# Where the tiles that TensorE reads lie in SBUF: multiples of 256 bytes instead of multiples of 32

## The chip, the core and the metric

The kernel runs on one core of a Trainium2 chip. The metric is device time in microseconds of one execution of the whole program; three executions of the kernel before were timed.

## What is computed

One layer of a hybrid decoder trunk: u is the RMS-normed input (16 meta tokens and 2,048 real ones, 1,024 features); one projection of u gives all inputs of two branches, a Mamba-2 scan (SSD) and gated linear attention (GLA), and the gates that merge them; then come the branch projections, the gated sum, the output projection and a last RMS norm.

```python
u = rmsnorm(hres, norm_w)
proj = jnp.einsum('bld,dn->bln', u, w_in)
z, xbc, dt_raw, q, k, v, g_gla, a_lr, merge_g = split_cols(proj, IN_WIDTHS)
...
y_m, s_m = ssd_chunked(xs[:, :m], dt[:, :m], a, bm[:, :m], cm[:, :m], N_META, s0)
y_r, _ = ssd_chunked(xs[:, m:], dt[:, m:], a, bm[:, m:], cm[:, m:], SSD_CHUNK, s_m)
...
o_r, _ = gla_chunked(q[:, m:], k[:, m:], v[:, m:], log_a[:, m:], GLA_CHUNK, st_m)
...
branch_proj = jnp.einsum('blnc,ncd->blnd', branches, w_branch)
gates = jax.nn.sigmoid(merge_g.reshape(b, l, N_BRANCH, D_MODEL))
merged = jnp.sum(gates * branch_proj, axis=2)
return hres + jnp.einsum('bld,de->ble', merged, w_out)
```

## The kernel before

**Matrix products.** Nearly all products are made from fp32 values split in two: a high half rounded to fp32r and a low half, the rest. A tile holds both halves side by side, `[P, 2, n]`, and `accum` (L212 to L216) makes three matmuls of them: high by high (L214), high by low (L215), low by high (L216). The stationary operand has 128 columns, the moving one up to 512. Each matmul loads its own weights.

**First phase.** The 2,048 tokens go in four blocks of 512; block 0 also holds the 16 meta tokens, so its tiles have 528 columns and the real tokens start at column 16. u of a block is eight tiles (one for each 128 features): blocks 1 and 3 use tiles named `uo`, blocks 0 and 2 tiles named `ue`, which have room for 528 columns in each half (`u_tile`, L267). `proj_feat` (L218) streams u past weights (moving u, stationary `whl`), `proj_tok` (L230) streams weights past u. Block 0's projections over all 528 columns go in two segments of 264 (L407), each in a PSUM bank of its own. The scans of both branches run beside the projections; their small products read tiles named `act`, `sq`, `c1`, `tok4`, `kdt`, `atp`, `bt`.

**Second phase.** Gates, branch projections and the output projection are done with seven products of sums and differences for eight (a Strassen-like scheme). For each pair of halves, `prep_a` (L1160) splits a stationary tile `a`, `prep_b` (L1112) a moving tile: `b6`, `b7`, `b5`, `b3`, `b4`, or, for products 1 and 2, one of the `ue` tiles again. `product` (L1168) runs four k-steps of three matmuls of 512 columns, in the order of products 1, 2, 6, 7, 5, 3, 4, each for two row groups: 168 matmuls for two row groups in all.

**Order.** TensorE's and SyncE's instructions run in the order in which the code is written (a manual schedule); those of the other engines are placed by a scheduler that models their times.

**Addresses.** Tiles come from pools. Left of the free gap, the pools follow each other upward from the end of the scratch for software DMAs (16 KiB a partition); right of it, downward from the top of SBUF. A tile starts on a multiple of 32 bytes; nothing more is asked for. So where a tile lies past a multiple of 256 bytes follows from the sizes of all pools ahead of it. For the tiles that TensorE reads most:

| Tile | read as | start past a multiple of 256 bytes: first half / second half |
|---|---|---|
| `uo` (blocks 1, 3) | moving and stationary | 96 / 96 |
| `ue` (blocks 0, 2, products 1 and 2), even and odd tiles | moving and stationary | 160 / 224 and 32 / 96 |
| `whl` (weights of the first phase) | moving and stationary | 96 / 96 |
| `a` (second phase) | stationary | 160 / 160 |
| `b6` | moving | 160 / 160 |
| `b7`, `b5`, `b3`, `b4` | moving | 224 / 224 |
| `sq`, `c1`, `kdt`, `atp`, `ot` | both | 32 |
| `act` | both | 32, 96, 160 or 224 |

In block 0 the real tokens add 64 bytes to this (16 columns), and the second segment adds 1,056 bytes, 32 past a multiple of 256.

**Software DMAs.** Eight DMAs of the whole program are issued by GpSimd (L346, block 0's u to DRAM). GpSimd also makes the low halves of the weights (L177, L190), which TensorE waits for.

Of the kernel before, what the change touches and what calls it, by code (L numbers as in the profile page):

```python
# [8 lines left out]
F32 = mybir.dt.float32  # L9
# [34 lines left out]
def trunk_kernel(ctx: ExitStack, tc: tile.TileContext, xm, xmt, w_feat, w_tok, w_v3, w_zm, w_br, w_o,  # L44
# [11 lines left out]
    base = ctx.enter_context(tc.tile_pool(name="base", bufs=1))  # L56
    wdram = ctx.enter_context(tc.tile_pool(name="wdram", bufs=1, space=bass.MemoryType.DRAM))
    dpool = ctx.enter_context(tc.tile_pool(name="dpool", bufs=2, space=bass.MemoryType.DRAM))
    mhalf = base.tile([P, 4], F32, name="mhalf")
    nc.vector.memset(mhalf, -0.5)  # L60


# [61 lines left out]
    def pool1(name, bufs):  # L124
        return first.enter_context(tc.tile_pool(name=name, bufs=bufs, side="right"))

    bpool, wk, sm, const = pool1("bpool", 1), pool1("wk", 2), pool1("sm", 4), pool1("const", 1)
    pj = ctx.enter_context(tc.tile_pool(name="pj", bufs=3, space=bass.MemoryType.PSUM))
    pt = ctx.enter_context(tc.tile_pool(name="pt", bufs=3, space=bass.MemoryType.PSUM))
    pc = ctx.enter_context(tc.tile_pool(name="pc", bufs=2, space=bass.MemoryType.PSUM))  # L130

    def bank(pool, tag):
        return mk(pool, [P, 512], F32, tag)
# [3 lines left out]
    ident = cst[:, 0, :]  # L137
    tri = cst[:, 1, :]
    tris = cst[:, 2:4, :]
    pv = const.tile([P, 118], F32, name="pv")  # L140
    norm_w = pv[:, 0:8]
    conv_w = pv[:, 8:72].rearrange("p (t k) -> p t k", k=4)
    conv_b = pv[:, 72:88]
# [121 lines left out]


    def u_tile(b):  # L267
        return mk(uodd, [P, 2, BLK], F32R, "uo") if b % 2 else mk(ueven, [P, 2, META + BLK], F32R, "ue")

    def load_u(b):  # L270
        m0 = META if b == 0 else 0
        row0 = META - m0 + b * BLK
        tt = m0 + BLK
        u = []

        def rows_load(r0, n, i=None):
            xt = mk(wk, [P, D], F32, "tok4", bufs=NT4) if i is None else mk(spool, [P, META + BLK], F32, "acc")[:, :BLK]
            nc.sync.dma_start(xt[:n], xm[r0:r0 + n, :] if i is None else xm[r0:r0 + n, i * BLK:(i + 1) * BLK])
            return xt

        def rstd_rows(ss, n):
            r = mk(sm, [P, 1], F32, "rs1")
            nc.vector.tensor_scalar(r[:n], ss[:n], 1.0 / D, EPS, op0=ALU.mult, op1=ALU.add)
            done = nc.gpsimd.tensor_tensor(r[:n], r[:n], mhalf[:n, 0:1], op=ALU.pow)
            return (r, done) if m0 else r

        def rows_rstd(r0, n, vector):
            ss = mk(sm, [P, 1], F32, "ss")
            xt = rows_load(r0, n)
            if vector:  # L290
                nc.vector.scalar_tensor_tensor(xt[:n], xt[:n], 1.0, xt[:n], op0=ALU.mult, op1=ALU.mult,
                                               accum_out=ss[:n])
            else:
                nc.scalar.activation(xt[:n], xt[:n], AF.Square, accum_out=ss[:n])
            return rstd_rows(ss, n)

        rs = []
        if m0:
            rm_s = rows_rstd(0, META, True)
            for c in range(NCH):  # L300
                rs.append(rows_rstd(META + b * BLK + c * P, P, c % 2))
        else:
            for c in range(NCH):
                s2 = mk(sm, [P, 2], F32, "ss2")
                for i in range(2):
                    xt = rows_load(META + b * BLK + c * P, P, i)
                    nc.scalar.activation(xt, xt, AF.Square, accum_out=s2[:, i:i + 1])
                    if i == 0:
                        yield
                ss = mk(sm, [P, 1], F32, "ss")  # L310
                nc.vector.tensor_tensor(ss, s2[:, 0:1], s2[:, 1:2], op=ALU.add)
                rs.append(rstd_rows(ss, P))
                yield
        if m0:
            rs.append(rm_s)
            first_rows.append(rs[NCH - 1][1])
            rs = [r for r, _ in rs]
            nc.sync.dma_start(cst[:, :2], cf32[:, :2])
            nc.sync.dma_start(pv, pvec)
            for q in range(NWR):  # L320
                raws[f"zm_{q}"] = load_raw(w_zm[:, q * 288:(q + 1) * 288])
        rb = bank(pt, "pt")
        for c in range(NCH):
            nc.tensor.matmul(rb[:, c * P:(c + 1) * P], rs[c].to_broadcast([P, P]), ident, start=True, stop=True)
        rbs = [(rb, m0, BLK)]
        if m0:
            rm = bank(pt, "pt")
            nc.tensor.matmul(rm[:, :META], rs[NCH][:META].to_broadcast([META, P]), ident[:META, :META],
                             start=True, stop=True)
            rbs = [(rm, 0, META)] + rbs  # L330
        else:
            rbc = mk(spool, [P, 3 + META + BLK], F32, "cin")[:, :BLK]
            nc.scalar.activation(rbc, rb, AF.Copy)
            rbs = [(rbc, 0, BLK)]
            yield
        lows = []
        for kt in range(KT):
            xk = (mk(wk, [P, META + BLK], F32, "act", bufs=NACT) if m0 else mk(spool, [P, META + BLK], F32, "acc"))[:, :tt]
            nc.sync.dma_start(xk, xmt[:, kt, row0:row0 + tt])
            with tc.issue_after(lows[kt - 2].ins) if m0 and kt > 1 else nullcontext():  # L340
                for ps, a, n in rbs:
                    nc.vector.scalar_tensor_tensor(xk[:, a:a + n], xk[:, a:a + n], norm_w[:, kt:kt + 1], ps[:, :n],
                                                   op0=ALU.mult, op1=ALU.mult)
            u.append(u_tile(b)[:, :, :tt])
            nc.scalar.activation(u[kt][:, 0], xk, AF.Copy)
            (nc.gpsimd if m0 else nc.scalar).dma_start(u_left[b][kt], xk[:, m0:])  # L346
            lows.append(nc.vector.tensor_tensor(u[kt][:, 1], xk, u[kt][:, 0].bitcast(F32), op=ALU.subtract))
            if m0:
                first_low[:] = lows[:2][-1:]
            yield  # L350
        return u
# [30 lines left out]
    msk = const.tile([P, NMSK, P], U8, name="msk")  # L382

    def late_constants():
        w2r = mk(wk, [P, META + BLK], F32, "act", bufs=NACT)[:48, :512]
        for i in range(3):
            nc.sync.dma_start(w2r[16 * i:16 * i + 16, :], gw2)
        nc.scalar.activation(w2, w2r, AF.Copy)
        nc.vector.tensor_tensor(w2[32:48], w2r[32:48], w2[32:48].bitcast(F32), op=ALU.subtract)
        mstg = mk(wk, [P, D], F32, "tok4", bufs=NT4)[:, :NMSK * P]  # L390
        nc.sync.dma_start(mstg, cmsk)
        nc.vector.tensor_copy(msk.rearrange("p l t -> p (l t)"), mstg)
# [4 lines left out]
    def new_block(b, u):  # L397
# [1 line left out]
        o.b, o.u = b, u  # L399
        o.m0 = META if b == 0 else 0  # L400
        o.tt = o.m0 + BLK
        o.segs_all = [(0, o.tt // 2), (o.tt // 2, o.tt // 2)] if b == 0 else [(0, BLK)]
        o.segs_real = [(o.m0, BLK)]
        o.starts = [o.m0 + c * P for c in range(NCH)]
        o.chunks = ([(0, META)] if o.m0 else []) + [(a, P) for a in o.starts]
# [61 lines left out]

    def gates(o):
        m0, tt, chunks, g_all = o.m0, o.tt, o.chunks, o.g_all
        ast = (mk(wk, [P, META + BLK], F32R, "act", bufs=NACT) if m0 else mk(wk, [P, BLK], F32R, "sq", bufs=NSQ))[:48, :tt]  # L470
        for a, n in ([(0, META), (m0, BLK)] if m0 else [(0, BLK)]):
            ps = bank(pt, "pt")
            for i, (ca, cn) in enumerate(chunks):
# [5 lines left out]
            nc.scalar.activation(ast[:16, a:a + n], ps[:16, :n], AF.Copy)  # L479
        yield  # L480
        for h2 in range(0, GH, 2):
            gmt = mk(wk, [P, 2, META + BLK], F32, "tok4", bufs=NT4)
            for h in (h2, h2 + 1):
                gm = gmt[:, h % 2, :tt]
                gb = gate_b[:, h:h + 1]
# [101 lines left out]
    def proj_conv(o, g):  # L587
        tt = o.tt
        feats = o.feats[g] = []
        for j in range(4):  # L590
# [10 lines left out]
            for k in range(3):  # L601
                convd[:] = [nc.vector.scalar_tensor_tensor(acc, cin[:, k:k + tt], hcw[:, ti, k:k + 1], acc,  # L602
                                                           op0=ALU.mult, op1=ALU.add)]
            f = mk(wk, [P, META + BLK], F32, "act", bufs=NACT)
            nc.scalar.activation(f[:, :tt], acc, AF.Tanh)
            nc.vector.scalar_tensor_tensor(f[:, :tt], f[:, :tt], 1.0, acc, op0=ALU.add, op1=ALU.mult)
            feats.append(f)
# [136 lines left out]

    def proj_qk(o, h):
        t0 = T_GLA + 4 * h
        qs = mk(wk, [P, META + BLK], F32, "act", bufs=NACT)
        ps, = proj_feat(f"g{t0}", w_feat[t0], o.segs_real, o.mov)
        evicted[:] = [nc.scalar.activation(qs[:, :BLK], ps, AF.Copy, scale=QSCALE)]
        yield  # L750
        kf = mk(wk, [P, META + BLK], F32, "act", bufs=NACT)
        for ps, (a, n) in zip(proj_feat(f"g{t0 + 1}", w_feat[t0 + 1], o.segs_all, o.mov), o.segs_all):
            evicted[:] = [nc.scalar.activation(kf[:, a:a + n], ps[:, :n], AF.Copy)]
        o.qk[h] = qs, kf
        yield
# [34 lines left out]
    def gla_scan(o, h, last=False):  # L790
# [5 lines left out]
        k = kf[:, m0:tt]  # L796
        grc = gr.rearrange("p (c t) -> p c t", t=P)

        kd = mk(wk, [P, META + BLK], F32, "act", bufs=NACT)
        gl = mk(sm, [P, NCH + 1], F32, "gl")  # L800
        with behind() if m0 else nullcontext():
            nc.scalar.activation(gl[:, :NCH], grc[:, :, P - 1], AF.Copy, scale=ITEMP)
# [7 lines left out]
        nc.vector.tensor_tensor(kd[:, :tt], kd[:, :tt], kf[:, :tt], op=ALU.mult)  # L810
        egl = mk(sm, [P, NCH], F32, "egl")
        nc.scalar.activation(egl, gl[:, :NCH], AF.Exp)
        qg = mk(wk, [P, META + BLK], F32, "act", bufs=NACT)[:, :BLK]
        nc.scalar.activation(qg, gr, AF.Exp, scale=ITEMP)
        nc.vector.tensor_tensor(qg, qg, q, op=ALU.mult)

# [639 lines left out]
        k += 1  # L1456
    ordered.close()
    first.close()
    bpl.update({p: pool2(f"bops{p}", 4, side="right") for p in (7, 5, 3, 4)})
    opl, spl = pool2("outs", 1, side="right"), pool2("small", 4, side="right")  # L1460
    bt_raws["all"] = opl, "br", 4
# [106 lines left out]
```

## Time and profile before

| | |
|---|---|
| median of 3 timed executions | 2237.41 us (2236.06 to 2238.92) |
| profiled execution: span from first to last instruction | 2236.0 us |
| first phase / second phase in it | up to about 1454 us / from there on |
| instructions | 34,965, of them 11,789 matmuls as the profile counts them |
| DMA | 517.95 MB, mean 232 GB/s |

The page names no other time of the profiled execution than its span. PE is TensorE's matmuls, PEld its weight loads, DVE VectorE, ACT ScalarE, POOL GpSimd, SP SyncE. A row of a timeline has the start in us, the duration in us, engine, source line, operation, the tile written and the tiles read, the shape, and how many instructions were merged in the row. Rows of a list of groups have the count behind an x, then the busy time in us and the mean of one in ns.

### The profile page before, as it was taken

How to read it: one execution, taken by the hardware profiler on the slowest of the kernel's cores; microseconds unless marked ns; L12 is line 12 of the kernel's file. 1: busy time of each engine (PE TensorE's matmuls, PEld its weight loads, DVE VectorE, ACT ScalarE, POOL GpSimd, SP SyncE). 2: the span in 40 equal slices, each digit the busy share in tenths (PEclk: the TensorE clock that was granted, in tenths of full speed). 3: DMA queues.
4: the chain of work that ended last, by engine and by line, in shares of the span. 5: the costliest groups of instructions: out<-in, count | busy, mean ns of one | idle time of the engine just before them, and what ended most of it. 6: DMA issues, size and time to landing. Idle time of an engine off the chain costs nothing.

```text
span 2236.0 us, 34965 instructions
## 1 busy us (share of the span) xinstructions
PE 2209.7 (99%) x11789; PEld 1896.8 (85%) x11789; DVE 1568.4 (70%) x2935; ACT 1187.0 (53%) x2767; POOL 689.2 (31%) x689
## 2 busy tenths in 40 slices
PE   7999999999999999999999999999999999999998
PEld 7999999888888888888988888878888888888887
DVE  5776776677567676567677666774689854789876
ACT  5666655575445466445465454464644545554544
POOL 5444432223212122221212100066233374323341
PEclk9999999999999999999999999999999999999999
DMA  9777775767788667778677664386768866777753
GB/s 318 246 229 240 266 267 192 239 211 237 240 253 258 211 213 236 239 248 269 208 216 230 212 214 157 125 276 202 240 221 288 303 221 212 247 279 248 251 181 120
DMA packets 313699, 517.95 MB, mean 232 GB/s; under 512 B 28080, under 2 KB 162480, under 8 KB 313520
## 3 DMA queue, kind: packets, MB, share of 16 engines
q1 hardware_dynamic: 247008, 419.89, 58.5%
q10 hardware_dynamic: 65872, 93.74, 11.5%
q8 instruction: 92, 1.51, 0.3%
q0 software_dynamic: 640, 2.10, 0.2%
q14 instruction: 87, 0.71, 0.1%
HBM read 368.42 MB, written 147.19 MB: 231 GB/s over the span
## 4 chain that ended last, share of the span: by engine, by line
PE 72%; DMA 1%; DVE 1%; ACT 1%; POOL 0%; issue 0%; POOLq 0%; SPq 0%; ACTq 0%; DVEq 0%
PE pj L214 15%; PE pj L216 15%; PE pj L215 15%; PE pt L214 4%; PE pt L215 4%; PE pt L216 4%; PE pc L216 2%; PE pc L214 2%; PE pc L215 2%; PE pc L691 2%; PE pc L852 1%; PE pc L692 1%; PE pc L960 1%; PE pc L694 1%; PE pt L666 1%; DMA acc<-in_xmt 1%
## 5 line engine op out<-in xcount | busy, mean ns | idle before, releaser
L214 PE MATMUL pj<-ue,whl 128*128 128x264 f32 (+1 forms) x672 | 235.4, 350 | 1.2 <-ACT acc L598 1.2
L216 PE MATMUL pj<-ue,whl 128*128 128x264 f32 (+1 forms) x672 | 229.7, 342 | 0.0
L215 PE MATMUL pj<-ue,whl 128*128 128x264 f32 (+1 forms) x672 | 228.8, 341 | 0.0
L214 PE MATMUL pj<-uo,whl 128*128 128x512 f32 x512 | 205.8, 402 | 0.0
L216 PE MATMUL pj<-uo,whl 128*128 128x512 f32 x512 | 200.2, 391 | 0.0
L215 PE MATMUL pj<-uo,whl 128*128 128x512 f32 x512 | 199.5, 390 | 0.0
L214 PE MATMUL pj<-b,a 128*128 128x512 f32 (+1 forms) x484 | 189.0, 391 | 0.5 <-DVE io L1283 0.5
L216 PE MATMUL pj<-b,a 128*128 128x512 f32 (+1 forms) x484 | 188.9, 390 | 0.0
L215 PE MATMUL pj<-b,a 128*128 128x512 f32 (+1 forms) x484 | 187.6, 388 | 0.0
L602 DVE SCALAR_TENSOR_TENSOR acc<-cin,hcw,acc 128x512 f32<-128x512 f32 (+1 forms) x192 | 157.9, 823 | 39.8 <-ACT acc L598 38.6
L83 POOL TENSOR_TENSOR wr<-wr 128x256 f32<-128x256 f32 x80 | 65.9, 823 | 373.7 <-DMA wr<-y 157.2
L1165 DVE TENSOR_TENSOR a<-ar,a 128x512 fp32r<-128x512 f32 x160 | 136.0, 858 | 61.3 <-ACT a L1164 60.5
L1136 POOL TENSOR_TENSOR as<-ar,ar 128x512 f32<-128x512 f32 x38 | 60.8, 1600 | 371.7 <-DMA ar<-in_w_br 185.9
L214 PEld LDWEIGHTS pj<-ue,whl 128*128 128x128 f32 x672 | 126.4, 188 | 16.7 <-ACT acc L598 1.6
L216 PEld LDWEIGHTS pj<-ue,whl 128*128 128x128 f32 x672 | 126.5, 188 | 14.9
L215 PEld LDWEIGHTS pj<-ue,whl 128*128 128x128 f32 x672 | 126.5, 188 | 14.7
L177 POOL TENSOR_TENSOR whl<-wr,whl 128x512 fp32r<-128x512 f32 (+1 forms) x76 | 96.2, 1274 | 126.0 <-ACT whl L175 80.6
L1199 ACT ACTIVATE sn<-pj 128x512 f32<-128x512 f32 x118 | 69.9, 592 | 121.7 <-PE pj L216 84.4
L1165 DVE TENSOR_TENSOR a<-as,a 128x512 fp32r<-128x512 f32 x120 | 100.6, 840 | 45.0 <-ACT a L1164 42.0
L1164 ACT ACTIVATE a<-ar 128x512 fp32r<-128x512 f32 x160 | 98.8, 624 | 58.1 <-PE pt L216 32.7
L214 PE MATMUL pt<-b,a 128*128 128x512 f32 x320 | 125.7, 393 | 0.0
L215 PE MATMUL pt<-b,a 128*128 128x512 f32 x320 | 125.3, 392 | 0.0
(335 smaller groups left out, 6456.8 us busy)
## 6 DMA issues: line engine op xcount, KB each, us to landing
whl<-k_s SPq DMA_DIRECT2D x96, 512.0 KB, 3.8
whl<-k_g SPq DMA_DIRECT2D x96, 512.0 KB, 4.2
whl<-k_v SPq DMA_DIRECT2D x36, 512.0 KB, 4.0
wr<-in_w_feat SPq DMA_DIRECT2D x64, 256.0 KB, 4.5
k_s<-whl SPq DMA_DIRECT2D x32, 512.0 KB, 3.9
cb<-cumd SPq DMA_DIRECT2D x64, 256.0 KB, 5.1
y<-gg ACTq DMA_DIRECT2D x64, 256.0 KB, 4.0
k_g<-whl SPq DMA_DIRECT2D x32, 512.0 KB, 3.8
```

The lines of the kernel that those rows point to most:

```text
L83: nc.gpsimd.tensor_tensor(o, x, y, op=ALU.subtract)
L177: nc.gpsimd.tensor_tensor(hl[:, 1], raw, hl[:, 0].bitcast(F32), op=ALU.subtract)
L214: nc.tensor.matmul(ps, sh, mh, start=first, stop=False, **kw)
L215: nc.tensor.matmul(ps, sh, ml, start=False, stop=False, **kw)
L216: nc.tensor.matmul(ps, sl, mh, start=False, stop=last, **kw)
L602: convd[:] = [nc.vector.scalar_tensor_tensor(acc, cin[:, k:k + tt], hcw[:, ti, k:k + 1], acc, op0=ALU.mult, op1=ALU.add)]
L666: nc.tensor.transpose(ps[:, j * P:(j + 1) * P], f[:, a:a + P], ident)
L691: nc.tensor.matmul(py[:, h * 64:(h + 1) * 64], dm[:, h], xdt[:, h], start=True, stop=True)
L1136: nc.gpsimd.tensor_tensor(s1, a21, a22, op=ALU.add)
L1164: nc.scalar.activation(t[:, 0], src, AF.Copy)
L1165: latest[:] = [nc.vector.tensor_tensor(t[:, 1], src, t[:, 0].bitcast(F32), op=ALU.subtract)]
L1199: nc.scalar.activation(sn, self.ps[n, "a"], AF.Copy)
```

## The change

It makes every tile that TensorE reads start on a multiple of 256 bytes, in both halves, by padding: `ue` tiles get 576 columns a half instead of 528, `act` tiles 576 instead of 528, the tiles of `gates` 544 instead of 528; four small pads fill pools up. Block 0's two segments become 256 and 272 columns, so that the second starts 1,024 bytes in. For the room, the scratch of software DMAs goes from 16 KiB to 4 KiB a partition. After it the starts of the tiles in the table above are all 0 past a multiple of 256. In block 0 the real tokens still start 64 bytes past that. `g_all` and `alr` (start 32) stay as they were; TensorE reads only `alr` of them, in a few small transposes a block.

```diff
-    mhalf = base.tile([P, 4], F32, name="mhalf")
+    mhalf = base.tile([P, 32], F32, name="mhalf")[:, :4]
...
+    mk(bpool, [P, 8], F32, "pad")
+    mk(spool, [P, 16], F32, "pad", bufs=1)
...
+    def act_tile(dt=F32):
+        return mk(wk, [P, 64 + BLK], dt, "act", bufs=NACT)
...
-    pv = const.tile([P, 118], F32, name="pv")
+    pv = const.tile([P, 128], F32, name="pv")[:, :118]
...
-        return mk(uodd, [P, 2, BLK], F32R, "uo") if b % 2 else mk(ueven, [P, 2, META + BLK], F32R, "ue")
+        return mk(uodd, [P, 2, BLK], F32R, "uo") if b % 2 else mk(ueven, [P, 2, 64 + BLK], F32R, "ue")
...
-        o.segs_all = [(0, o.tt // 2), (o.tt // 2, o.tt // 2)] if b == 0 else [(0, BLK)]
+        o.segs_all = [(0, BLK // 2), (BLK // 2, META + BLK // 2)] if b == 0 else [(0, BLK)]
...
-            gmt = mk(wk, [P, 2, META + BLK], F32, "tok4", bufs=NT4)
+            gmt = mk(wk, [P, 2, 32 + BLK], F32, "tok4", bufs=NT4)
...
-            f = mk(wk, [P, META + BLK], F32, "act", bufs=NACT)
+            f = act_tile()
...
+    top = pool2("top", 1, side="right")
+    mk(top, [P, 56], F32, "pad")
...
-    nc = _bacc.Bacc("TRN2", target_bir_lowering=False, num_devices=1)
+    nc = _bacc.Bacc("TRN2", target_bir_lowering=False, num_devices=1, dynamic_dma_scratch_size=4096)
```

All other places that make an `act` tile use `act_tile` in the same way. Lines of the changed kernel stand 5 lower from there on, and later 7.

TensorE, the first projection of block 0 over all columns, before (pj_621 and pj_622 are the two PSUM banks, ue_313 and ue_321 two tiles of u):

```order
L214 MATMUL pj_621<-ue_313,whl_572 128x264
L215 MATMUL pj_621<-ue_313,whl_572 128x264
L216 MATMUL pj_621<-ue_313,whl_572 128x264
L214 MATMUL pj_622<-ue_313,whl_572 128x264
L215 MATMUL pj_622<-ue_313,whl_572 128x264
L216 MATMUL pj_622<-ue_313,whl_572 128x264
```

and the same place of the changed kernel:

```order
L219 MATMUL pj_623<-ue_315,whl_574 128x256
L220 MATMUL pj_623<-ue_315,whl_574 128x256
L221 MATMUL pj_623<-ue_315,whl_574 128x256
L219 MATMUL pj_624<-ue_315,whl_574 128x272
L220 MATMUL pj_624<-ue_315,whl_574 128x272
L221 MATMUL pj_624<-ue_315,whl_574 128x272
```

The same matmuls stand in the same order, with 256 and 272 columns for 264 and 264; the rest of TensorE's rows are as before, and so are all of GpSimd's and SyncE's. ScalarE, the evictions of block 0's convolution inputs (cin, acc) beside the weights' high halves (whl), before:

```order
L598 ACTIVATE acc_848<-pj_784,hcb,hcw 128x264
L189 ACTIVATE whl_949<-wr_951 128x512
L189 ACTIVATE whl_1021<-wr_1023 128x512
L605 ACTIVATE act_858<-acc_848 128x528
L595 ACTIVATE cin_1213<-tails 128x3
L597 ACTIVATE cin_925<-pj_861 128x264
```

and now:

```order
L603 ACTIVATE acc_850<-pj_786,hcb,hcw 128x272
L194 ACTIVATE whl_951<-wr_953 128x512
L610 ACTIVATE act_860<-acc_850 128x528
L600 ACTIVATE cin_1215<-tails 128x3
L194 ACTIVATE whl_1023<-wr_1025 128x512
L602 ACTIVATE cin_927<-pj_863 128x256
```

One split of a weight moved behind the tanh (L605, now L610) of the convolution before it. A few such moves in block 0 are all that changed in ScalarE's order; VectorE's changed only in the widths.

More of the change, by code (lines that the diff above doesn't have):

```diff
@@ L337, in load_u @@
         for kt in range(KT):
-            xk = (mk(wk, [P, META + BLK], F32, "act", bufs=NACT) if m0 else mk(spool, [P, META + BLK], F32, "acc"))[:, :tt]
+            xk = (act_tile() if m0 else mk(spool, [P, META + BLK], F32, "acc"))[:, :tt]
             nc.sync.dma_start(xk, xmt[:, kt, row0:row0 + tt])
@@ L384, in late_constants @@
     def late_constants():
-        w2r = mk(wk, [P, META + BLK], F32, "act", bufs=NACT)[:48, :512]
+        w2r = act_tile()[:48, :512]
         for i in range(3):
@@ L469, in gates @@
         m0, tt, chunks, g_all = o.m0, o.tt, o.chunks, o.g_all
-        ast = (mk(wk, [P, META + BLK], F32R, "act", bufs=NACT) if m0 else mk(wk, [P, BLK], F32R, "sq", bufs=NSQ))[:48, :tt]
+        ast = (act_tile(F32R) if m0 else mk(wk, [P, BLK], F32R, "sq", bufs=NSQ))[:48, :tt]
         for a, n in ([(0, META), (m0, BLK)] if m0 else [(0, BLK)]):
@@ L746, in proj_qk @@
         t0 = T_GLA + 4 * h
-        qs = mk(wk, [P, META + BLK], F32, "act", bufs=NACT)
+        qs = act_tile()
         ps, = proj_feat(f"g{t0}", w_feat[t0], o.segs_real, o.mov)
@@ L750, in proj_qk @@
         yield
-        kf = mk(wk, [P, META + BLK], F32, "act", bufs=NACT)
+        kf = act_tile()
         for ps, (a, n) in zip(proj_feat(f"g{t0 + 1}", w_feat[t0 + 1], o.segs_all, o.mov), o.segs_all):
@@ L797, in gla_scan @@
         grc = gr.rearrange("p (c t) -> p c t", t=P)
-        kd = mk(wk, [P, META + BLK], F32, "act", bufs=NACT)
+        kd = act_tile()
         gl = mk(sm, [P, NCH + 1], F32, "gl")
@@ L812, in gla_scan @@
         nc.scalar.activation(egl, gl[:, :NCH], AF.Exp)
-        qg = mk(wk, [P, META + BLK], F32, "act", bufs=NACT)[:, :BLK]
+        qg = act_tile()[:, :BLK]
         nc.scalar.activation(qg, gr, AF.Exp, scale=ITEMP)
```

## The prediction

> **What bounds the kernel now.** I read the page from the top: the busy shares, then the chain, then the waits of TensorE, and after these the starts of single matmuls, because nothing else decides here.
>
> ```profile
> PE 2209.7 (99%) x11789; PEld 1896.8 (85%) x11789; DVE 1568.4 (70%) x2935; ACT 1187.0 (53%) x2767; POOL 689.2 (31%) x689
> PE 72%; DMA 1%; DVE 1%; ACT 1%; POOL 0%; issue 0%; POOLq 0%; SPq 0%; ACTq 0%; DVEq 0%
> ```
>
> ```profile
> PE pt L324 <- DMA cst<-in_cf: 10.1, 1, 10.1
> PE pc L691 <- DVE sq L682: 2.0, 2, 1.6
> PE pj L214 <- ACT ue L345: 1.5, 1, 1.5
> ```
>
> TensorE is busy 99% of the span; the chain that ended last is made of matmuls; the longest wait (10.1 us) is the first load, and the next ones together are a few us. So the time is a sum of distances between starts of matmuls, and only what changes these distances changes the time. A matmul's duration in the lists (some 390 ns) is a modelled one that overlaps the next; I therefore use starts, first and last of a run, divided by the number between.
>
> In the second phase (from 1467 us on) TensorE waits for nothing but half a microsecond near the end, and the work repeats every 168 matmuls of 512 columns:
>
> ```profile
> 1660.29 0.39 PE L214 MATMUL pj<-b,a 128*128 128x512 f32 x1
> ...
> 1698.87 0.39 PE L214 MATMUL pj<-b,a 128*128 128x512 f32 x1
> ```
>
> 38.58 us / 168 = **229.6 ns** each. Now a run of the same shape in block 1, whose u lies in tiles "uo", and one in block 2, whose u lies in tiles "ue":
>
> ```profile
> 490.44 0.39 PE L214 MATMUL pt<-whl,uo 128*128 128x512 f32 x1
> ...
> 495.88 0.39 PE L214 MATMUL pt<-whl,uo 128*128 128x512 f32 x1
> ```
>
> ```profile
> 840.46 0.40 PE L214 MATMUL pt<-whl,ue 128*128 128x512 f32 x1
> ...
> 845.33 0.39 PE L214 MATMUL pt<-whl,ue 128*128 128x512 f32 x1
> ```
>
> 24 matmuls in 5.44 us are **226.7 ns** each; 21 in 4.87 us are **231.9 ns**. Engine, line, shape, weights and pools are the same. What differs is where the operands start: uo and whl both at 96 past a multiple of 256 bytes, in both halves; ue at 160 or 32 in the first half and 224 or 96 in the second (4,224 bytes a tile, halves 2,112 apart). The whole blocks say it again, by the first matmul of blocks 1, 2 and 3:
>
> ```profile
> 390.89 0.30 PE L214 MATMUL pj<-whl,uo 128*128 128x288 f32 x1
> 739.65 0.29 PE L214 MATMUL pj<-whl,ue 128*128 128x288 f32 x1
> 1091.79 0.30 PE L214 MATMUL pj<-whl,uo 128*128 128x288 f32 x1
> ```
>
> Block 1 takes 348.8 us and block 2, with the same matmuls, 352.1.
>
> **The change part by part.** The program keeps its instructions; the order on TensorE, GpSimd and SyncE is the same row for row. What moves is the address of nearly every operand, the width of block 0's two segments, and a few evictions.
>
> *Second phase.* Its operands start at 224 (b7, b5, b3, b4), 160 (b6, a) and the four values of ue; after the change all start at 0. One pair there is equal already, b6 with a, 160 and 160 in both halves. It comes behind products of ue, and its first 12 matmuls (1698.87 to the first row here) take 230.8 ns, then it settles:
>
> ```profile
> 1701.64 0.39 PE L214 MATMUL pj<-b,a 128*128 128x512 f32 x1
> ...
> 1704.36 0.40 PE L214 MATMUL pt<-b,a 128*128 128x512 f32 x1
> ```
>
> 12 in 2.72 us, again 226.7 ns, at another start than uo's 96. So I take 226.7 for equal starts, wherever they lie. The matmuls:
>
> ```profile
> L214 PE MATMUL pj<-b,a 128*128 128x512 f32 x476 | 186.7, 392 | 0.0
> L214 PE MATMUL pt<-b,a 128*128 128x512 f32 x320 | 125.7, 393 | 0.0
> L215 PE MATMUL pj<-ue,a 128*128 128x512 f32 x160 | 63.0, 394 | 0.0
> L216 PE MATMUL pc<-ue,a 128*128 128x512 f32 x160 | 63.2, 395 | 0.0
> ```
>
> 1,116 on one line, three lines (high by high, high by low, low by high): 3,348. Times 229.64 - 226.67 = 2.97 ns: **-9.9 us**. All of it is on the path, since nothing else is waited for there. VectorE is next: the window rows give it 269.7 of 383 us and, in the last part, 292.8 of 386, so a phase shorter by 1.3% does not reach it.
>
> ```profile
> 1467.00:1850.00 383.00, 383.00 (x1670) 313.25 (x1669) 269.74 (x348) 194.97 (x347) 181.84 (x142) 1.00 0.74 252
> 1850.00:2236.00 386.00, 378.39 (x1659) 309.68 (x1657) 292.83 (x424) 187.72 (x359) 126.92 (x92) 1.00 0.65 219
> ```
>
> *Blocks 1 and 3* have equal starts already (96) and get others (0): nothing, if only equality counts. *Block 2* becomes like block 1: 3.4 us less, of which a wait that only block 2 has (1.1 us, below) is not the layout's. I take **-2.2 us**.
>
> ```profile
> PE pt L446 <- DVE ecu L443: 1.1, 1, 1.1
> ```
>
> *Block 0* keeps unequal starts: its real tokens stand 16 columns in, 64 bytes past the start of a tile that now is at 0. Its 288 matmuls of 512 columns go from four mixed starts to a pair 64 bytes apart. Such a pair, 224 with 160, are the products of b7, b5 and b3 by a in the second phase:
>
> ```profile
> 1705.06 0.39 PE L214 MATMUL pt<-b,a 128*128 128x512 f32 x1
> ...
> 1717.42 0.39 PE L214 MATMUL pj<-b,a 128*128 128x512 f32 x1
> ```
>
> 54 in 12.36 us, 228.9 ns against 231.9: -0.9 us. Its segments of 264 and 264 columns become 256 and 272:
>
> ```profile
> 54.89 0.28 PE L214 MATMUL pj<-ue,whl 128*128 128x264 f32 x1
> ...
> 56.71 0.28 PE L214 MATMUL pj<-ue,whl 128*128 128x264 f32 x1
> ```
>
> ```profile
> 712.82 0.28 PE L214 MATMUL pj<-whl,uo 128*128 128x256 f32 x1
> ...
> 714.97 0.28 PE L214 MATMUL pj<-whl,uo 128*128 128x256 f32 x1
> ```
>
> 264 columns take 121.3 ns (15 in 1.82 us), 256 with equal starts 119.4 (18 in 2.15 us). A column more costs (226.7 - 119.4) / 256 = 0.42 ns, so 272 take 126.1. The pair goes from 242.6 to 245.5, +2.9 ns, 480 pairs: +1.4 us. A few evictions move by a place with it (ACT is busy 53%); nothing. Block 0 together: **+0.5 us**, between -1 and +2.
>
> *The scratch* for software DMAs shrinks to a quarter. Only block 0's eight stores of u use it:
>
> ```profile
> L346 POOL DMA_DIRECT2D u<-act x8: 539/554/759, 14.0 to 25.9; - x8
> ```
>
> Each holds GpSimd 0.55 us. Behind one that waits for room stands the subtraction that makes a weight's low half, and TensorE waits for that. No row shows such a wait. Its bounds are nothing, and one landing, 4.6 us in the median for this line, for each store that finds no room. I take nothing, by the even 0.54 to 0.76 us of the eight.
>
> *Sum:* 2236.0 - 9.9 - 2.2 + 0.5 = 2224.4 us of span. The page gives that execution no time beside its span; the timed runs' median is 2237.4, 1.4 us above it. Forecast: **2226 us** (2225.8), -0.5%. With block 0's and block 2's bounds, and 228 instead of 226.7 ns in the second phase (-5.5 us), that case spans 2220 to 2232.
>
> **The rivals.**
>
> *The start itself counts, not only its equality.* A matmul of 512 columns at 226.7 ns has 13 ns that are not columns (512 x 0.42 = 214). All starts of these operands are odd multiples of 32 bytes, but for the second segments of block 0, so the trace hardly shows what a multiple of 64 or more would give. If part of the 13 ns is a first or last piece of a line that only a displaced operand has, it goes in all 9,700 or so such matmuls, blocks 1 and 3 too. For it: 13 ns stand there at both widths, as a cost per operand would. Against it: in the 264-column run above every second three start at multiples of 64, and at 121.3 ns it stands only 2 or 3 below 264 x 0.42 + 13 = 124. Half of it, 16 columns or 64 bytes, 6.7 ns: 9,700 x 6.7 = 65 us, so 2161. All of it: 6,800 x 13 = 88 us, and some 8 ns for the 2,800 narrower ones, down to the 111 ns that a pass of 128 columns takes here (8 in 0.89 us), 22 us: 2116.
>
> ```profile
> 633.44 0.89 PE pc L852 x8
> ```
>
> The page "TensorE: Matmul & The Clock Gate" of the Trainium skill, section "Wait — 56ns, not 53.3ns?", gives 512 columns as 215.7 ns back to back; the trace's best run is 11 ns above it. By that figure as a floor, the 3,348 of the second phase alone would lose 47 us, an estimate from that page.
>
> *Nothing.* The difference between uo and ue could come from which buffer is read against which, in steps that alignment to 256 does not touch, or the second phase's 229.6 from its own three PSUM pools. For it: the tiles b have the same start in both halves and still take 228.9. Against it: that start is 64 bytes from a's, and b6, where it is not, settles at 226.7. Time 2237, within 4.5 us.
> The page "SBUF — State Buffer" of the Trainium skill, section "Specifications (TRN2)", has lines of 16 bytes and a penalty for crossing to a new one. Every operand before starts on a multiple of 32 and runs contiguously, so by that rule this change moves nothing; the 226.7 against 231.9 ns above already speak against it as the whole story.
>
> *Slower: equal starts collide.* Weights are loaded while the matmul before streams. If both now begin on the same position of every 256 bytes and position 0 is a bad one, all matmuls take what the worst run takes, 231.9 ns: +2.3 ns on 3,348 and +5.2 on some 2,100 of blocks 1 and 3, which are at 226.7 now: 7.7 + 11 us, and the segments' 1.4: 2258. It decides from a second phase above 230 ns a matmul. For it: at 256 columns equal starts are the slower ones, 119.4 against
>
> ```profile
> 216.57 0.28 PE L214 MATMUL pj<-whl,ue 128*128 128x256 f32 x1
> ...
> 218.69 0.28 PE L214 MATMUL pj<-whl,ue 128*128 128x256 f32 x1
> ```
>
> 117.8 ns for mixed ones (18 in 2.12 us). Against it: at 512 columns equal starts are the fastest that the trace has.
>
> **How the numbers follow.** Equality counts, 2220 to 2232, likeliest 2226: 0.52. The start itself counts: 0.24, of it half the 13 ns or less (2160 to 2220) 0.12, more 0.12. Nothing: 0.13. Slower: 0.11. Below 0.2% (4.5 us, about what a measurement of this kernel can tell from no change) nothing is told apart. So faster 0.76, same 0.13, slower 0.11. The range leaves out the deeper half of the first rival and most of the slower one: 2160 to 2243; the likeliest case's own is 2220 to 2232.
>
> **What would show it.** Right: the period of 168 matmuls in the second phase at 38.1 us (now 38.58), blocks 1, 2 and 3 equally long near 348.8 us, and no new wait of TensorE. Blocks 1 and 3 clearly shorter than now would mean the first rival; a period unchanged, the second; above 38.7 us, the third. A wait of TensorE for a weight's low half before 60 us would mean the scratch. The pairs of block 0 at 245 ns would show the segments' price.

## The result, and the profile after

| | before | changed |
|---|---|---|
| median of the timed executions | 2236.73 us (4 runs, 2233.17 to 2238.92) | 2222.82 us (4 runs, 2221.41 to 2224.33) |
| ratio, 95% interval | | 0.9938 (0.9924 to 0.9952) |
| profiled execution, span | 2236.0 us | 2220.6 us |

The change saves 13.9 us, 0.6%. The profiled execution of the changed kernel itself took 2222.45 us, 1.85 more than its span. If the same 1.85 us are added to the span of before, its profiled execution took about 2237.8 us, an estimate, and lay 1.1 above its median, while the changed one lay 0.4 below its own. So the two spans differ by 15.4 us and the medians by 13.9.

The page of the changed kernel, busy shares and chain: TensorE is still the only engine that decides, and all the others have the load that they had. (The shares of the chain that the page of before lists add up to only 75%, so its 72% for TensorE and the 90% here can't be compared.)

```profile
PE 2194.1 (99%) x11789; PEld 1893.9 (85%) x11789; DVE 1564.9 (70%) x2935; ACT 1186.6 (53%) x2767; POOL 694.4 (31%) x689
PE 90%; DVE 2%; DMA 2%; issue 1%; ACT 1%; POOL 0%; SPq 0%; POOLq 0%; ACTq 0%; DVEq 0%
```

Its timeline at the same two matmuls of the second phase, 168 apart, that the prediction used (`accum` is now L219 to L221):

```profile
1651.15 0.39 PE L219 MATMUL pj<-b,a 128*128 128x512 f32 x1
...
1689.23 0.39 PE L219 MATMUL pj<-b,a 128*128 128x512 f32 x1
```

The period was 38.58 us and is 38.08, 226.7 ns a matmul instead of 229.6. The run of 21 matmuls in block 2, which was at 231.9 ns, and the first matmuls of blocks 1, 2 and 3:

```profile
836.38 0.39 PE L219 MATMUL pt<-whl,ue 128*128 128x512 f32 x1
...
841.13 0.39 PE L219 MATMUL pt<-whl,ue 128*128 128x512 f32 x1
```

```profile
389.57 0.29 PE L219 MATMUL pj<-whl,uo 128*128 128x288 f32 x1
...
737.75 0.30 PE L219 MATMUL pj<-whl,ue 128*128 128x288 f32 x1
...
1085.05 0.30 PE L219 MATMUL pj<-whl,uo 128*128 128x288 f32 x1
```

The run is at 226.2 ns. Block 1 takes 348.2 us (348.8 before), block 2 takes 347.3 (352.1): the block that was the slow one has become like its neighbour. TensorE's waits now:

```profile
PE pt L329 <- DMA cst<-in_cf: 9.0, 1, 9.0
PE pc L219 <- DVE c L953: 1.6, 2, 1.2
PE pj L219 <- ACT ue L350: 1.5, 1, 1.5
PE pc L696 <- DVE sq L687: 1.5, 1, 1.5
PE pt L671 <- ACT g_all L496: 1.3, 1, 1.3
PE pj L219 <- ACT acc L603: 1.0, 1, 1.0
PE pj L219 <- ACT sn L1204: 0.9, 1, 0.9
```

Two of them, for `g_all` and for `sn`, are new among the long ones; block 2's wait for `ecu` is not there in this profile. The difference of the two spans by stretches, each taken between the starts of the same matmuls in both traces (the second phase from the matmul with index 8,400, counted from 0, to the last one; block 3 runs up to there and holds 1,955 matmuls, against 1,875 of block 1 and 1,872 of block 2, so its length is not to be compared with theirs):

| stretch | before | changed | difference | predicted |
|---|---|---|---|---|
| up to the first matmul of 288 columns | 14.5 | 13.4 | -1.0 | 0 |
| block 0 | 376.4 | 376.1 | -0.3 | +0.5 |
| block 1 | 348.8 | 348.2 | -0.6 | 0 |
| block 2 | 352.1 | 347.3 | -4.8 | -2.2 |
| block 3 | 360.7 | 360.8 | +0.1 | 0 |
| second phase | 776.1 | 767.6 | -8.6 | -9.9 |
| after the last matmul | 7.3 | 7.2 | -0.2 | 0 |
| span | 2236.0 | 2220.6 | -15.4 | -11.6 |

### The profile page after: what moved, and what is told of

It reads as the page before. It is cut to its first block, busy times and chain, and to the rows that moved or that the text cites. A ratio compares the mean times of both kernels' runs of the same rounds, so it can differ in the third digit from the quotient of the medians.

```text
span 2220.6 us, 34964 instructions
## 1 busy us (share of the span) xinstructions
PE 2194.1 (99%) x11789; PEld 1893.9 (85%) x11789; DVE 1564.9 (70%) x2935; ACT 1186.6 (53%) x2767; POOL 694.4 (31%) x689
## 3 DMA queue, kind: packets, MB, share of 16 engines
q10 hardware_dynamic: 65872, 93.74, 11.4%
## 4 chain that ended last, share of the span: by engine, by line
PE 90%; DVE 2%; DMA 2%; issue 1%; ACT 1%; POOL 0%; SPq 0%; POOLq 0%; ACTq 0%; DVEq 0%
PE pj L219 20%; PE pj L221 20%; PE pj L220 20%; PE pt L221 4%; PE pt L219 4%; PE pt L220 4%; PE pc L696 2%; PE pc L219 2%; PE pc L220 2%; PE pc L221 2%; PE pc L857 2%; PE pc L697 1%; PE pc L699 1%; PE pc L965 1%; PE pt L671 1%
## 5 line engine op out<-in xcount | busy, mean ns | idle before, releaser
L219 PE MATMUL pj<-ue,whl 128*128 128x512 f32 (+2 forms) x672 | 235.1, 350 | 1.1 <-ACT acc L603 1.0
L221 PE MATMUL pj<-ue,whl 128*128 128x512 f32 (+2 forms) x672 | 228.5, 340 | 0.0
L220 PE MATMUL pj<-ue,whl 128*128 128x512 f32 (+2 forms) x672 | 228.3, 340 | 0.0
L219 PE MATMUL pj<-uo,whl 128*128 128x512 f32 x512 | 205.5, 401 | 0.0
L221 PE MATMUL pj<-uo,whl 128*128 128x512 f32 x512 | 200.0, 391 | 0.0
L219 PE MATMUL pj<-b,a 128*128 128x512 f32 (+1 forms) x484 | 187.5, 388 | 1.4 <-ACT sn L1204 0.9
L221 PE MATMUL pj<-b,a 128*128 128x512 f32 (+1 forms) x484 | 187.4, 387 | 0.0
L1141 POOL TENSOR_TENSOR as<-ar,ar 128x512 f32<-128x512 f32 x38 | 66.1, 1739 | 365.0 <-DMA ar<-in_w_br 163.2
L219 PEld LDWEIGHTS pj<-ue,whl 128*128 128x128 f32 x672 | 126.5, 188 | 16.2 <-ACT acc L603 1.5
L221 PEld LDWEIGHTS pj<-ue,whl 128*128 128x128 f32 x672 | 126.2, 188 | 14.5
L221 PE MATMUL pt<-b,a 128*128 128x512 f32 x320 | 124.5, 389 | 0.0
```

Of the source, the lines that this page charges most:

```text
L219: nc.tensor.matmul(ps, sh, mh, start=first, stop=False, **kw)
L220: nc.tensor.matmul(ps, sh, ml, start=False, stop=False, **kw)
L221: nc.tensor.matmul(ps, sl, mh, start=False, stop=last, **kw)
L1141: nc.gpsimd.tensor_tensor(s1, a21, a22, op=ALU.add)
```

## The experiments

The trace bears out that equal starts are faster, but the two layouts differ in everything at once: the start itself, the equality of the two halves, multiples of 256, the segments and the scratch. The runs take these apart. A "three" below is the high by high, high by low and low by high matmul of `accum`, start to start: 680 ns a three is 226.7 ns a matmul. "Equal" is short for: all operands start at the same place past a multiple of 256 bytes.

**The price of a start, alone.** TensorE runs matmuls from tiles of which only the starts differ; no other engine works beside it. The core of the kernel:

```python
for w, mh, ml, sh, sl in CONFIGS:      # columns; starts of the moving and stationary halves
    for n in range(REPS):              # REPS = 20
        ...
        a, b = mv[:, k, mh // 4:mh // 4 + w], mv[:, k + 1, ml // 4:ml // 4 + w]
        x, y = st[:, k, sh // 4:sh // 4 + P], st[:, k + 1, sl // 4:sl // 4 + P]
        nc.tensor.matmul(ps[:, :w], x, a, ...)
        nc.tensor.matmul(ps[:, :w], x, b, ...)
        nc.tensor.matmul(ps[:, :w], y, a, ...)
```

> The whole computation is left out: 52 streams of 60 matmuls each, three by three as in accum (high by high, high by low, low by high), 512 columns wide unless said, the output filled with one tile. Each stream has its own starts past a multiple of 256 bytes for the two moving and the two stationary halves. Equality theory (only differences between starts count): five streams with all four starts at 0, 32, 64, 96 and 128 all take 680 ns a three; moving 64 bytes from stationary 687; other differences 683 to 698; 256 columns with equal starts 360, with moving and stationary 64 apart about 340. Rival (a start at a multiple of 64 or more is better by itself): the streams at 0, 64 and 128 are below those at 32 and 96, by up to 20 ns a three. Second rival (13 ns are a fixed cost of a matmul): 320, 384, 448 and 504 columns have the columns' time plus 13 ns each, 1.25 ns for 3 columns; the equality theory alone says nothing on them.

Its timeline, first and last row of 27 matmuls for three streams of 512 columns: all operands at 32, all at 128, and the moving ones displaced by 4 bytes from the stationary ones:

```profile
30.09 0.39 PE L70 MATMUL ps<-mv,st 128*128 128x512 f32 x1
...
36.21 0.39 PE L70 MATMUL ps<-mv,st 128*128 128x512 f32 x1
...
70.99 0.39 PE L70 MATMUL ps<-mv,st 128*128 128x512 f32 x1
...
77.11 0.39 PE L70 MATMUL ps<-mv,st 128*128 128x512 f32 x1
...
84.90 0.40 PE L70 MATMUL ps<-mv,st 128*128 128x512 f32 x1
...
91.29 0.40 PE L70 MATMUL ps<-mv,st 128*128 128x512 f32 x1
```

6.12 us / 27 = 226.7 ns at 32 and at 128, and so at 0, 64 and 96; with 4 bytes between them 6.39 us, 236.7 ns. All other displacements, of both moving halves, of one of them or of one stationary half, lay between 228.9 and 234.4 ns, 687 to 703 a three, and so up to 5 above the 683 to 698 that were expected. So at 512 columns it is equality, not the place, and one half displaced is enough to lose it. The period is 256 bytes: 128 bytes between moving and stationary cost 6.7 ns a matmul, while the moving tiles of the equal streams stand 2,560 bytes apart and the stationary ones 768, so that these differ by odd and by even multiples of 256, and every three takes 680. With that the rival "the start itself counts" is gone: the 13 ns that are not columns by the prediction's 0.42 ns a column stand at every equal start. The expectation's second rival, 13 ns as a fixed cost of each matmul, fits 320 and 384 columns (440 and 520 ns a three) and not 448 and 504 (620 and 680, against 603 and 674 with 0.42 ns a column and 13 ns).

**The same in the kernel.** Every tile that TensorE reads is moved to 32 bytes past a multiple of 256, so that none is on one and all are still equal:

```diff
+    mk(base, [P, 8], F32, "pad")
...
-    mk(bpool, [P, 8], F32, "pad")
+    mk(bpool, [P, 64], F32, "pad")
...
-    mk(top, [P, 56], F32, "pad")
+    mk(top, [P, 112], F32, "pad")
```

> The changed kernel with every tile that TensorE reads moved by 32 bytes, so that all start 32 past a multiple of 256. Equality theory: as the changed kernel, 2223 us, 0.6% under the kernel before, second phase 226.7 ns a matmul. Rival (the multiple of 256 counts): the second phase goes back toward 229 ns or more, 2232 to 2240 us.

2223.66 us, ratio 0.9938 (0.9926 to 0.9951): the changed kernel's time. Its second phase has the same period, 38.08 us:

```profile
1648.47 0.39 PE L220 MATMUL pj<-b,a 128*128 128x512 f32 x1
...
1686.55 0.39 PE L220 MATMUL pj<-b,a 128*128 128x512 f32 x1
```

The multiple of 256 is a way to make starts equal and nothing more.

**One half of u displaced.** As the changed kernel, but the second half of the `ue` tiles starts 64 bytes past the first:

```diff
-        return mk(uodd, [P, 2, BLK], F32R, "uo") if b % 2 else mk(ueven, [P, 2, 64 + BLK], F32R, "ue")
+        return mk(uodd, [P, 2, BLK], F32R, "uo") if b % 2 else mk(ueven, [P, 1216], F32R, "ue")[:, :1184].rearrange("p (i c) -> p i c", i=2)
```

> The changed kernel, but the second half of each ue tile starts 64 bytes past a multiple of 256 (blocks 0 and 2, products 1 and 2); all else at 0. Theory that both halves must be equal: 960 matmuls of the second phase and 1056 of block 2 go from 226.7 to 230 to 232 ns each, +7 to +11 us, 2230 to 2234 us; block 2 longer than block 1 by 3 to 5 us. Rival (only moving against stationary of the same matmul counts, and the low moving half alone is displaced): a third of it, 2225 to 2226 us.

2233.42 us, ratio 0.9988 (0.9979 to 0.9997): about three quarters of the gain are gone by these 64 bytes. The first matmuls of blocks 2 and 3, and the two of the second phase:

```profile
740.08 0.30 PE L219 MATMUL pj<-whl,ue 128*128 128x288 f32 x1
...
1091.38 0.30 PE L219 MATMUL pj<-whl,uo 128*128 128x288 f32 x1
...
1658.99 0.39 PE L219 MATMUL pj<-b,a 128*128 128x512 f32 x1
...
1697.36 0.39 PE L219 MATMUL pj<-b,a 128*128 128x512 f32 x1
```

Block 2 is back at 351.3 us, and the period at 38.37, in the middle. Only the products that read `ue` lost: in the second phase the distances from start to start of these add up to 223.4 us here, against 218.5 in the changed kernel and 222.7 before; those of `b` by `a` to 542.4, as in the changed kernel (542.5; before 546.8). So the second phase's gain comes in about equal parts from `ue` and from `b`.

**The scratch alone.** The kernel before, with nothing but the smaller scratch:

```diff
-    nc = _bacc.Bacc("TRN2", target_bir_lowering=False, num_devices=1)
+    nc = _bacc.Bacc("TRN2", target_bir_lowering=False, num_devices=1, dynamic_dma_scratch_size=4096)
```

> The kernel before with the 4 KiB scratch alone; all starts past a multiple of 256 stay as they were. Theory (the scratch costs nothing): 2237 us, the eight GpSimd stores 0.54 to 0.76 us each. Rival (stores wait for room): up to 4.6 us more for each that waits, 2241 us and more, with longer stores in the trace.

2236.92 us, ratio 0.9997 (0.9987 to 1.0006). The eight stores on GpSimd take what they took:

```profile
L346 POOL DMA_DIRECT2D u<-act x8: 539/554/759, 14.1 to 25.4; - x8
```

It also shows how much a stretch varies without any change of layout. Block 2 of this run:

```profile
739.89 0.29 PE L214 MATMUL pj<-whl,ue 128*128 128x288 f32 x1
...
1090.90 0.30 PE L214 MATMUL pj<-whl,uo 128*128 128x288 f32 x1
```

351.0 us, 1.1 less than in the profile of before.

**Is equality the best arrangement?** The same microbenchmark with the moving high half at 0 and the other three halves at every combination of 0, 64, 128 and 192.

> The computation is left out: TensorE alone runs streams of 45 matmuls (threes as in accum) from operands at chosen starts. First stream and last: all equal, 512 columns. Then, at 512 and at 256 columns, the moving high half stays at 0 and the moving low half, the stationary high half and the stationary low half stand at every combination of 0, 64, 128 and 192 bytes past a multiple of 256. Last, 264 and 272 columns with both stationary halves displaced by 0 to 192. Theory 'equality is the best at 512 columns': only the all-equal combination settles at 680 ns a three, every one of the other 63 stays between 685 and 710. Rival 'some other arrangement is as good or better, for example the two stationary halves so placed that each weight load and the stream beside it never meet': at least one of the 63 shows 680 or less. At 256 columns the first theory has nothing to say; the first microbenchmark had 360 for equal starts and 340 for a moving pair displaced by 64, and I expect 340 (3 x 113 ns) to be the floor, reached by several combinations. 272 columns: 375 with equal starts, and 264 the same 360 as 256.

At 512 columns only the equal one settles at 680 ns a three; the other 63 lie between 686.4 and 706.7. At 256 columns equal starts take 360 and are among the slowest; the other combinations take 340 to 363, most of them 353 or more, and 340 is reached by two of the 64, fewer than expected.

**The segments.** Two kernels: the changed one with the segments exchanged, and with the old ones back.

```diff
-  o.segs_all = [(0, BLK // 2), (BLK // 2, META + BLK // 2)] if b == 0 else [(0, BLK)]
+  o.segs_all = [(0, META + BLK // 2), (META + BLK // 2, BLK // 2)] if b == 0 else [(0, BLK)]    # exchanged
+  o.segs_all = [(0, o.tt // 2), (o.tt // 2, o.tt // 2)] if b == 0 else [(0, BLK)]                # old
```

> As the changed kernel, but block 0's two segments are 272 and 256 columns in this order, so that the second starts 1,088 bytes in, 64 past a multiple of 256, with 256 columns. Theory 'the relative start and the width set the price, as in the microbenchmark': the 256-column three of a pair, 64 bytes apart from its weights, falls from 360 to 340 ns and the 272-column three stays near 375, so a pair of threes goes from 733 to about 715 ns; 160 pairs, -2.9 us against the changed kernel: 2220, ratio to the kernel before near 0.992. Rival 'a three that follows one of another start pays again (the equal state takes three threes to settle)': the pair stays at 725 to 740 ns and the time at 2222 to 2224.

> As the changed kernel, but with the old segments of 264 and 264 columns in block 0 (the second starts 1,056 bytes in, 32 past a multiple of 256). My prediction had the new segments 2.9 ns dearer for each pair of single matmuls, 8.7 ns for a pair of threes. If so, a pair of threes takes 724 to 728 ns here against 733, and the span is 0.7 to 1.4 us shorter than the changed kernel's, which one profile can just show in block 0 and a time can't. Rival 'the new segments are the cheaper ones, since both start on a multiple of 256': the pair takes over 735 ns.

2222.46 us for the first, ratio 0.9943 (0.9929 to 0.9956), and one execution of 2221.13 for the second; no difference that a time can show. The timelines of the same seven pairs of threes in block 0 show one: the changed kernel, then the exchanged segments, then the old ones.

```profile
123.73 0.36 PE L219 MATMUL pj<-ue,whl 128*128 128x256 f32 x1
...
128.94 0.28 PE L219 MATMUL pj<-ue,whl 128*128 128x256 f32 x1
```

```profile
122.44 0.37 PE L219 MATMUL pj<-ue,whl 128*128 128x272 f32 x1
...
127.61 0.29 PE L219 MATMUL pj<-ue,whl 128*128 128x272 f32 x1
```

```profile
123.40 0.37 PE L219 MATMUL pj<-ue,whl 128*128 128x264 f32 x1
...
128.60 0.28 PE L219 MATMUL pj<-ue,whl 128*128 128x264 f32 x1
```

744, 739 and 743 ns a pair of threes; the median of all 160 pairs is 733, 727 and 731 (before 729), and the 960 matmuls together take 121.5, 120.7 and 121.0 us from start to start (before 120.8). The exchange gave 0.8 us of the 2.9 that the microbenchmark's 340 had promised: its 256-column threes took 352 ns in the median. This miss belongs to the first theory; the rival named there had the sizes right: each of these threes follows one of another width and start, and pays for the change. That this is the reason is argued, not shown. The old segments are the cheaper ones, as the prediction had it, but by 2 ns a pair of threes, where 724 to 728 against 733 had been expected, and by 0.5 us in all, about a third of the 1.4 that the prediction gave.

**Which equality?** Operands that change from matmul to matmul, to separate a matmul's own two operands from the moving operand and the weights that are loaded while it streams.

> The computation is left out: TensorE alone runs streams of 72 matmuls whose operands change from one matmul to the next, every stream at 512 and at 256 columns. A pair (m, s) is the start of the moving and of the stationary operand past a multiple of 256. Theory A, equality within a matmul counts: at 512 columns the streams (0,0) (64,64) in turn, in threes of each or in a row of three starts, run at 226.7 ns like (0,0) alone, and (0,64) (64,0) in turn runs above 228.5. Theory B, equality of a moving operand with the weights of the next matmul counts, which are loaded while it streams: the reverse; (0,64) (64,0) and (0,64) (64,128) (128,0) run at 226.7, since each next stationary operand starts where the present moving one does, while (0,0) (64,64) in turn runs above 228.5, and (0,128) (64,0) (128,64), which is unequal both ways, too. Rival C, both must be equal all the time: every stream but the constant (0,0) stays above 228.5. The streams (0,64), (64,0), (0,192), (192,0) come twice each behind other streams: if only the difference counts and not what ran before, (0,64) equals (192,0) and both repeats agree within 1 ns; in the earlier microbenchmarks a displacement of the same size gave 687 and 700 ns a three, so I expect that they need not agree.

In a pair (m, s), m is the start of the moving operand and s that of the stationary one. The timeline, 36 matmuls from row to row, each row two merged matmuls: a constant (0, 0); then (64, 0), (0, 192), and (0, 192) a second time, behind other streams.

```profile
18.79 0.62 PE L67 MATMUL ps<-mv,st 128*128 128x512 f32 x2
...
26.95 0.62 PE L67 MATMUL ps<-mv,st 128*128 128x512 f32 x2
...
152.11 0.62 PE L67 MATMUL ps<-mv,st 128*128 128x512 f32 x2
...
160.35 0.63 PE L67 MATMUL ps<-mv,st 128*128 128x512 f32 x2
...
168.60 0.62 PE L67 MATMUL ps<-mv,st 128*128 128x512 f32 x2
...
176.84 0.62 PE L67 MATMUL ps<-mv,st 128*128 128x512 f32 x2
...
251.66 0.63 PE L67 MATMUL ps<-mv,st 128*128 128x512 f32 x2
...
260.06 0.63 PE L67 MATMUL ps<-mv,st 128*128 128x512 f32 x2
```

8.16 us are 226.7 ns a matmul, 8.24 are 228.9, and the same operands a second time take 8.40, 233.3. Theories A and B both fall: (0,0) (64,64) in turn, equal within each matmul, takes 231.7, and (0,64) (64,0), equal with the next weights, 231.7 too. Only rival C is left, one start for all operands of a stream; it alone gave 226.7, in each of its three streams. What is unequal has more than one rate for the same starts, by what ran before it. At 256 columns this is larger still in proportion: (0, 64) took 117.8 ns the first time and 113.3 the second.

**A mix of all that seemed better.** The exchanged segments, and weights tiles of 576 columns a half, in which a weight stands 64 bytes further where that makes block 0's 512-column products equal, or those of 256 columns in blocks 1 to 3 unequal:

```diff
-        hl = mk(wpool, [P, 2, 512], F32R, "whl", bufs=4)[:, :, :n]
+        hl = mk(wpool, [P, 2, 576], F32R, "whl", bufs=4)[:, :, off:off + n]
...
-            h, lo = load_w(f"{key}_{half}", src[:, half * 512:(half + 1) * 512])
+            h, lo = load_w(f"{key}_{half}", src[:, half * 512:(half + 1) * 512], segs[0][0])
...
-                  load_w(f"{key}_{q}", src[:, q * per * width:(q + 1) * per * width]) for q in (q0, q0 + 1)]
+                  load_w(f"{key}_{q}", src[:, q * per * width:(q + 1) * per * width],
+                         16 if width == 256 and not starts[0] else 0) for q in (q0, q0 + 1)]
```

> As seg272, and weights tiles of 576 columns a half, so that a weight can stand 64 bytes further: it does so for block 0's 512-column products (their u starts at 64, so the starts become equal: 96 threes from 699 to 680 ns, -0.7 to -1.8 us) and for the 256-column products of blocks 1 to 3 (equal starts now, 360 ns a three; 64 apart 340 in the microbenchmark and in block 0: 96 threes, -1.9 us). With seg272's -0.8 that is -3.4 to -4.5 us against the changed kernel of the same call: about 2219, ratio to the kernel before 0.992. Rival: the engine's neighbours (waits for VectorE's and ScalarE's results) take part of it back, as 1.3 us of the second phase's 9.9 were: less than 2 us, not to be told from the changed kernel.

> The changed kernel once more, beside the mix, for a comparison on the same chip: 2222 to 2224, ratio 0.994 to the kernel before.

2222.85 us for the mix (ratio 0.9933, 0.9921 to 0.9946) and 2222.74 for the changed kernel beside it (0.9930, 0.9916 to 0.9943): the same, and not the 3.4 to 4.5 us less that were expected. The starts say why. Block 0's 288 products of 512 columns went from 67.1 to 66.7 us, and the 96 of 256 columns in block 1 and in block 2 from 11.7 to 11.5, 359 ns a three instead of 365 and not 340: the fast rate of unequal starts did not come. What was gained, some 1.8 us with the segments, is less than the waits vary. This is the list of the mix's waits; on the line of `c` the changed kernel beside it had 1.1 us:

```profile
PE pc L219 <- DVE c L954: 2.8, 4, 0.8
```

So no version was found that beats the changed kernel.

## Why the prediction was right, point by point

**What bounds the kernel:** right. A sum of distances between starts of matmuls went down, and nothing else moved much.

**Second phase, -9.9 us:** right in its matmuls. Leaving out the few distances that hold a wait, 3,344 starts after and 3,346 before are 226.69 and 229.65 ns apart: 2.96 ns, where 2.97 was predicted, 9.9 us over 3,348. What came back is 1.3 us, and the prediction had said that nothing would wait there. 1.0 us of it stands at one row of the changed kernel's timeline, behind the last matmul of the product before it:

```profile
1928.37 0.39 PE L221 MATMUL pt<-b,a 128*128 128x512 f32 x1
1929.62 0.50 PE L219 MATMUL pj<-b,a 128*128 128x512 f32 x1 [0.86 <-ACT sn L1204]
```

1.25 us stand between two starts instead of 0.23. The matmul waits until ScalarE has copied (to `sn`) the PSUM bank in which it goes on adding. VectorE's load was asked about in the prediction, ScalarE's was not. This wait was there again in the second profile of the changed kernel (1.3 us in three places) and not in that of the mix nor in that with the old segments, so it is no fixed price.

**Block 2, -2.2 us:** the right mechanism, with a term mis-sized. The 3.4 us between blocks 1 and 2 had been lessened by 1.1 for a wait for `ecu` that "is not the layout's". The wait is indeed not the layout's: it took 0.5 us in the profile of the smaller scratch, which has the old layout, and in the changed kernel nothing in the first profile and 0.6 in the second. But the 3.4 us were not the sum of this wait and the layout. The 1,056 products of 512 columns alone took 3.0 us more in block 2 than in block 1 (247.9 and 244.9 us, start to start), and the change took 3.25 us off them (to 244.6); the 96 products of 256 columns with weights moving take 0.3 back (11.4 to 11.7 us), as equal starts are the slower ones there. So the layout is worth 3.0 us in this block, where 2.2 was taken. The rest of the 4.8 that the first profiles show is waits, that for `ecu` above all. With the second profiles, 351.0 for the old layout and 348.4 for the new one (next rows, of the changed kernel's second profile), block 2 is 3.7 us shorter on the mean of two.

```profile
737.97 0.30 PE L219 MATMUL pj<-whl,ue 128*128 128x288 f32 x1
...
1086.35 0.30 PE L219 MATMUL pj<-whl,uo 128*128 128x288 f32 x1
```

**Blocks 1 and 3, nothing:** right; their 512-column products take 244.7 us after and 244.9 before in block 1, 244.6 and 244.8 in block 3. Most of block 1's 0.6 us lies in small transposes of its scans, whose waits differ from one execution to the next.

**Block 0, +0.5 us:** -0.3, within the -1 to +2 given, but in part by luck, since terms that the prediction did not have cancel. The 512-column products gave -0.5 (-0.9 predicted), the segments +0.7 (+1.4 predicted, and the old ones put back gave 0.5 of it). Left out was a term: block 0's other 768 products of 256 columns, 672 of them now 64 bytes apart, went from 94.0 to 92.1 us. They are the ones that the prediction's own rows, 119.4 ns equal and 117.8 mixed, had shown to be sensitive. Against these stands the wait for `g_all`, 1.3 us, at 73.9 us. Whether it belongs to the change stays open: it is in the second profile of the changed kernel (1.0 us) and in those of the displaced half, the old segments and the mix (0.9 to 1.1), but not in the one with all tiles at 32, nor with the exchanged segments, nor in either profile of the old layout. The stretch as a whole can't settle a term of half a microsecond: it took 377.3 us in the other profile of the old layout, 375.3 in the second of the changed kernel, and 372.5 with all tiles at 32, where most of the difference arises in the first 100 us.

**Scratch, nothing:** right, by a run of its own. The sign that the prediction named for the scratch, a wait for a weight's low half before 60 us, is in the first profile of the changed kernel once, with 0.28 us:

```profile
20.92 0.40 PE L220 MATMUL pj<-whl,ue 128*128 128x288 f32 x1 [0.28 <-POOL whl L182]
```

It is in no other profile with the smaller scratch, the kernel before with this alone among them, so it is no fixed price either.

**The other signs.** The period of 168 matmuls came out at 38.08 us (38.1 named). Blocks 1 and 2 are nearly equal, but at 348.2 and 347.3 us; block 3 can't be read this way, as its stretch holds more matmuls. "No new wait" did not hold (`g_all`, `sn`). The pairs of single matmuls in block 0, a third of a pair of threes, were named at 245 ns and have a median of 244.3, against 243.0 before: 1.3 ns dearer, where 2.9 was predicted.

**The sum** was -11.6 us of span; the profiles showed -15.4 and the medians -13.9. Of the rest, 1.0 us is the first load, 9.0 us here, which took 10.1 again in the second profile of the changed kernel, so it is not the change's; 2.6 us are block 2's, its waits included, 0.8 block 0's and 0.6 block 1's, and the waits of the second phase took 1.3 back.

**The rivals.** "The start itself counts" falls by the microbenchmark (226.7 ns at five starts) and by the kernel with all tiles at 32. The figure of 215.7 ns for 512 columns in the Trainium skill, "TensorE: Matmul & The Clock Gate", section "Wait — 56ns, not 53.3ns?", was reached by none of the microbenchmarks' streams; 226.7 was the best at any start. "Nothing" falls by the period. The rule of 16-byte lines of the Trainium skill, "SBUF — State Buffer", section "Specifications (TRN2)", would have every displacement by a multiple of 16 cost nothing; 16, 32 and 64 bytes cost 2 to 7 ns a matmul here, and 4 bytes cost the most, 10. "Equal starts collide" is wrong at 512 columns and true at 256, 360 ns a three, against 340 to 363 for unequal ones, about half of them at 353 or below; since only 32 threes in each block and some scan products run equal at that width, it costs little here.

**What stays open** is the mechanism inside. That equal starts give the fast rate at 512 columns is shown, in the kernel and by TensorE alone; why they do is not. The runs show when the rate is lost, not which port or buffer loses it: neither the equality within a matmul nor that with the next weights explains it, and the unequal streams' rate depends on what ran before.

## What to carry to other kernels

Where TensorE is busy all the time, compare distances between matmul starts, for the same shape, across tiles: two rates for one shape can point to the addresses, and a padding of tiles that gives all operands of a stream the same start past a multiple of 256 bytes, in both halves of a split value, was worth 1 to 2.5% of such streams at 512 columns here. Do not expect it at 256 columns, and do not tune for the fast rates of unequal starts, since they come and go with what runs before. When two stretches differ by a fraction of a percent, do not subtract a single wait from the difference and call the rest the layout's; add up the distances of the one shape that the change can touch. A second profile of the same layout moved a block by 1 us, while the sum over its 512-column products moved by less than 0.1.

## What the runs showed of the hardware that was not expected

- Widths, all starts equal, ns a three: 256 and 264 columns both 360, 272 375, 288 395, 320 440, 384 520, 448 620, 504 and 512 both 680. Against 0.42 ns a column, 448 columns (1.26 x 448 = 564) carry 56 ns more, 512 carry 35.
- The equal rate needs one to four threes to settle behind a stream of another start: 687, 697, 684, then 680 in the second microbenchmark; 696, 691, 697, 685, then 681 for `b6` behind `ue` in the kernel before (medians over its periods), so that only the second half of this product ran at 226.7 ns there. Short runs do not reach it.
- 4 bytes of displacement cost more than any other distance that was tried: 710 ns a three at 512 columns.
- At 256 columns the same operands ran at 113.3 or 117.8 ns, by what ran before.
